# Turning half of a on VectorE in 32x32 blocks instead of on TensorE, in a fused matmul-GELU-matmul

## The chip, the core and the metric

The kernel runs on one core of a Trainium2 chip. The metric is the device time of one execution in microseconds; below, "us" is always that. The core has a matrix engine (TensorE, PE in the profile, with its weight loads listed apart as PEld), a vector engine (VectorE, DVE), an activation engine (ScalarE, ACT), GpSimd (POOL) and SyncE (SP). Loads are issued by SyncE, which moves bytes as they are, or by GpSimd, which here also casts float32 to bfloat16 on the way. Each engine runs its own instructions in the order in which the program gives them.

## The reference

```python
def setup_inputs():
    m, k, n, p = 1024, 1024, 2048, 1024   # a: m x k, b: k x n, c: n x p, float32

def reference(a, b, c):
    h = np.matmul(a, b)
    h = 0.5 * h * (1 + np.tanh(np.sqrt(2 / np.pi) * (h + 0.044715 * h ** 3)))
    return np.matmul(h, c).astype(np.float32)
```

## The kernel before

The first product is computed transposed: h^T, 2048 rows in 16 tiles of 128, by 1024 columns in two halves of 512 (`h` = 0 and 1, rows 0 to 511 and 512 to 1023 of a). A product on TensorE takes a 128x128 block of b as weights (contraction row tile `k`, column tile `t`) and streams 512 columns of a transposed (`aT[:, h, k]`). Its partitions are the contraction, so a has to be turned: its contraction index must lie on the partitions.

Before the change, all of a is turned on TensorE. Four transposes of 128x128 make one 128x512 piece in PSUM, and VectorE copies it to `aT` (`turn`, L138 to L147). a comes in eight quarters (`h`, `q`): 512 rows by 256 columns, 512 KB of float32. Three of them, (0,0), (1,0) and (0,1), come as float32 on SyncE's queue and are cast by VectorE and ScalarE (`cast_a`); the other five come already cast on GpSimd's queue (`abq`, L86). b's first three row tiles come in the same way on SyncE's queue (`stb`, `cast_b`), the rest of b and all of c as bfloat16 on GpSimd's (L89 to L104). GpSimd's queue starts after a small gate instruction (L81) that waits for the first quarter of a.

The work falls into stages, written out by hand in one order for every engine (`manual_schedule`; nothing reorders it):

- The first stage (L229 to L287) computes h^T's column tiles 0 to 3, both halves, directly: `block(h, tiles, ks)` runs `mm1` (L112) over row tiles `ks`. The products of a row tile stand between the transposes of the next. Eight PSUM banks hold `ps[0, t]`, `ps[1, t]` and the transposes (`bank(7)`). When a half is summed, `gelu` on ScalarE writes it to `hT`.
- Then three rounds of one level of Strassen-Winograd's scheme (seven products for eight, class `Seven`, function `seven`, products on L212): `zero` (column tiles 4 to 7), `one` (8 to 15) and `two` (the second matmul with c). Their operands are sums and differences formed on VectorE (`t1` to `t4`, `s1` to `s4`, L170) in float32r. `zero.t1` needs row tiles 0 to 3 of `aT`, `zero.t2` and `zero.t3` row tiles 4 to 7; `zero.s1` needs columns 768 to 1023 of b, `b1[:, :, 768:]`, all eight row tiles.
- `zero`'s first products take `b1[:, 0:4]`, columns from 512 on, its second products `b1[:, 4:8]`; those columns are loaded by L98.

Slots are shared: `x1`, `x2`, `x3` hold staging tiles first and Strassen operands later.

Of the kernel before, what the change touches and what calls it, by code (L numbers as in the profile page):

```python
# [9 lines left out]
F32 = mybir.dt.float32  # L10
F32R = mybir.dt.float32r
BF16 = mybir.dt.bfloat16
AF = mybir.ActivationFunctionType
# [6 lines left out]
def kernel(ctx, tc, a, b, c, out):  # L20
    nc = tc.nc
# [3 lines left out]
    H = 512  # L25
    KT = K // 128
    NT = N // 128

    av = a.rearrange("(mt p) k -> p mt k", p=128)
    bv = b.rearrange("(kt p) n -> p kt n", p=128)  # L30
    cv = c.rearrange("(nt p) q -> p nt q", p=128)

    ctx.enter_context(tc.manual_schedule())
# [6 lines left out]
    def slot(tag, shape, dt, name):  # L40
        return big.tile(shape, dt, name=name, tag=tag)

    def bank(i, shape=(128, H), dt=F32, name="ps"):
        return pp.tile(list(shape), dt, name=name, tag=f"bank{i}", padded_shape=None)

    def pieces(tag, bufs, shape, dt, name):
        return small.tile(shape, dt, name=name, tag=tag, bufs=bufs)
# [4 lines left out]
    gate = consts.tile([128, 1], F32, name="gate")  # L52
    g = consts.tile([128, 1], F32, name="g")
# [5 lines left out]
    aT = slot("a", [128, 2, KT, H], BF16, "aT")  # L59
    b1 = slot("b1", [128, KT, 1024], BF16, "b1")  # L60
    b2 = slot("b2", [128, KT, 1024], BF16, "b2")
# [2 lines left out]
    KH = KT // 2  # L64
    stb = slot("x0", [128, KT, H], F32, "stb")
    sta = slot("x1", [128, 2, 2, 4, 256], F32, "sta")
    abq = slot("x3", [128, 4, 2, 4, 256], BF16, "abq")

    def a_part(h, q):
        return av[:, 4 * h:4 * h + 4, ds(q * 256, 256)]  # L70

    def b_part(q):
        return bv[:, 2 * q:2 * q + 2, 0:H]

    nc.sync.dma_start(out=sta[:, 0, 0], in_=a_part(0, 0))  # L75
    nc.sync.dma_start(out=stb[:, 0:2], in_=b_part(0))  # L76
    nc.sync.dma_start(out=sta[:, 1, 0], in_=a_part(1, 0))
    nc.sync.dma_start(out=sta[:, 0, 1], in_=a_part(0, 1))
    nc.sync.dma_start(out=stb[:, 2], in_=bv[:, 2, 0:H])

    nc.gpsimd.tensor_copy(gate, sta[:, 0, 0, 3, 0:1])  # L81
    nc.scalar.activation(g, warm[:, 0:1], AF.Gelu_apprx_tanh)


    def cast_load_a(h, q):
        nc.gpsimd.dma_start(out=abq[:, q, h], in_=a_part(h, q))  # L86

    def cast_load_b(q):
        nc.gpsimd.dma_start(out=b1[:, 2 * q:2 * q + 2, 0:H], in_=b_part(q))  # L89

    cast_load_a(1, 1)
    nc.gpsimd.dma_start(out=b1[:, 3, 0:H], in_=bv[:, 3, 0:H])
    for q in range(2, 4):
        cast_load_a(0, q)
        cast_load_b(q)
        cast_load_a(1, q)
    for k in range(0, KT, 4):
        nc.gpsimd.dma_start(out=b1[:, k:k + 4, H:], in_=bv[:, k:k + 4, ds(H, H)])  # L98
    for n in range(2):
        for k in range(0, KT, 4):  # L100
            nc.gpsimd.dma_start(out=b2[:, k:k + 4, ts(n, H)],
                                in_=bv[:, k:k + 4, ds(1024 + n * H, H)])
    for t in range(0, NT, 2):
        nc.gpsimd.dma_start(out=c_sb[:, t:t + 2], in_=cv[:, t:t + 2])  # L104

    def copy(eng, dst, src):
        if eng is nc.scalar:
            nc.scalar.activation(dst, src, AF.Copy)
        else:
            nc.vector.tensor_copy(dst, src)  # L110

    def mm1(p, t, h, ks):  # L112
        for k in ks:
            nc.tensor.matmul(p, b1[:, k, ts(t, 128)], aT[:, h, k],  # L114
                             start=(k == 0), stop=(k == KT - 1))

    def gelu(t, h, p):
        nc.scalar.activation(hT[h][:, t], p, AF.Gelu_apprx_tanh)  # L118

    ps = {(0, t): bank(t) for t in range(4)}  # L120
# [7 lines left out]
    def cast_a(h, q, *engs):  # L128

        ab = pieces("ab", 2, [128, 4, 256], BF16, "ab")  # L130
        for i, eng in enumerate(engs):
            w = 256 // len(engs)
            for j, e in enumerate(eng if isinstance(eng, tuple) else (eng,)):
                m = slice(2 * j, 2 * j + 2) if isinstance(eng, tuple) else slice(0, 4)
                copy(e, ab[:, m, ts(i, w)], sta[:, h, q][:, m, ts(i, w)])
        return ab

    def turn(h, q, i, ab):  # L138

        banks = i if isinstance(i, tuple) else (i,)  # L140
        pts = [bank(x, (128, 2, H), BF16, "pt") for x in banks]
        for n in range(2):
            pt = pts[n % len(pts)]
            for m in range(4):
                nc.tensor.transpose(pt[:, n, ts(m, 128)], ab[:, m, ts(n, 128)], ident)  # L145
            nc.vector.tensor_copy(aT[:, h, 2 * q + n], pt[:, n])  # L146
            yield  # L147

    def cast_b(k, *engs):
        c0 = 0  # L150
        for i, eng in enumerate(engs):
            w = (H - c0) if i == len(engs) - 1 else H // len(engs) // 128 * 128
            copy(eng, b1[:, k, ds(c0, w)], stb[:, k, ds(c0, w)])
            c0 += w

    def block(h, tiles, ks):
        for k in ks:
            for t in tiles:
                mm1(ps[h, t], t, h, (k,))
# [56 lines left out]
    def pair(i):  # L216
        x = slot(f"x{i}", [128, 2, 4, H], F32R, "x1")
        return x[:, 0], x[:, 1]
# [3 lines left out]
    def quarters(b, c0, w):  # L222
        return [[b[:, 0:4, ds(c0, w)], b[:, 4:8, ds(c0, w)]],
                [b[:, 0:4, ds(c0 + w, w)], b[:, 4:8, ds(c0 + w, w)]]]

    zero = Seven(4, quarters(b1, H, 256), BB, [None] * 4, [None] * 4, 2)
    one = Seven(4, quarters(b2, 0, H), BB, [None] * 4, zero.t)

    stir(256, 256, 256, 256, 256)  # L229
    tn = turn(0, 0, 4, cast_a(0, 0, nc.vector))  # L230
    next(tn)
    stir(128)
# [4 lines left out]
    ab = cast_a(1, 0, nc.vector, nc.scalar)  # L237
    block(0, range(4), (0,))
    block(0, range(2), (1,))
    for _ in turn(1, 0, (7, 6), ab):  # L240
        pass
    block(0, range(2, 4), (1,))
    ab = cast_a(0, 1, (nc.scalar, nc.vector), nc.vector)
# [3 lines left out]
    zero.t[0], zero.t[1] = pair(2)  # L247
    block(1, range(3), (0,))
    tn = turn(0, 1, 7, ab)
    next(tn)  # L250
    block(1, range(3), (1,))
    next(tn)
    zero.t1(4, 0)
    for q in range(1, 3):
        k = 2 * q
        block(0, range(4), (k,))
        tn = turn(1, q, 7, abq[:, q, 1])
        next(tn)
        block(0, range(4), (k + 1,))
        next(tn)  # L260
        zero.t1(4, q)
        block(1, range(3), (k,))
        tn = turn(0, q + 1, 7, abq[:, q + 1, 0])
        next(tn)
        block(1, range(3), (k + 1,))
        next(tn)
    zero.t1(4, 3)
    block(0, range(4), (6, 7))
    zero.t2(2, 0)
    for t in range(4):  # L270
        gelu(t, 0, ps[0, t])
    ps[1, 3] = bank(7)
    mm1(ps[1, 3], 3, 1, range(2))
    tn = turn(1, 3, 0, abq[:, 3, 1])
    next(tn)
    mm1(ps[1, 3], 3, 1, range(2, 5))
    next(tn)
    mm1(ps[1, 3], 3, 1, (5,))
    zero.t[2], x11 = pair(1)
    zero.t[3], x31 = pair(3)  # L280
    zero.plain_t(2, 0)
    zero.t3(2, 0)
    zero.t2(2, 1)
    block(1, range(3), (6, 7))
    mm1(ps[1, 3], 3, 1, range(6, 8))
    for t in range(4):
        gelu(t, 1, ps[1, t])  # L287

# [199 lines left out]
```

## Time and profile before

| | |
|---|---|
| median of 3 runs | 117.67 us (117.56 to 117.71) |
| span of the profiled execution, first to last instruction | 115.7 us |
| what lies around the span, if the profiled execution took the median | 2.0 us |
| TensorE busy | 111.1 us (96%), 542 matmuls and transposes |
| VectorE busy | 90.0 us (78%) |
| ScalarE busy | 51.4 us (44%) |
| granted TensorE clock | 1.00 |
| loads by GpSimd (q0) | 9.31 MB as bfloat16, 8672 packets |
| loads by SyncE and all stores (q1) | 6.56 MB, 4736 packets |

How to read it: the span runs from the first to the last instruction. "Busy" of TensorE counts pipelined matmuls, so 96% isn't 96% of peak. A line such as `L146 DVE COPY aT<-pt 128x512 bf16<-128x512 bf16 x16 | 6.7, 423` names the line of the program, the engine, the operation, the tile written and the tile read with their shapes, how many there are, their busy time in us and the mean of one in ns. The chain of waits follows the work that ended last back from the end, at each step to what released it; in order of time each of its lines is a start in us, a length in us and what it was. In the timeline each line is a start, a length, an instruction (or several alike), and in brackets how long the engine had been idle and what ended that. An answer for one source line gives durations in ns (smallest, median, largest), the first and last start in us, and for a load the time from issue to landing.

### The profile page before, as it was taken

The page shows a single profiled execution, that of the slowest core. Times are in us where ns is not written, and L with a number is a line of the kernel's source. Part 1 is how long each engine was busy: PE and PEld are TensorE (multiplying, and loading weights), DVE is VectorE, ACT ScalarE, POOL GpSimd, SP SyncE. Part 2 cuts the span into 40 slices and gives each one's busy share as a digit, 9 for nine tenths or more (in the row PEclk, how much of TensorE's full clock was granted, in tenths as well). Part 3 has the DMA queues.
Part 4 walks back from the last instruction along what each step waited for, and adds up shares of the span by engine and source line. Part 5 has one row for each costly group of instructions (what it writes and reads, how often), then busy time and mean ns, then how long its engine had stood idle before and what let it go on. Part 6 is the DMA issues. An engine that isn't in the chain of part 4 may idle for free.

```text
span 115.7 us, 1461 instructions
## 1 busy us (share of the span) xinstructions
PE 111.1 (96%) x542; PEld 77.1 (67%) x542; DVE 90.0 (78%) x107; ACT 51.4 (44%) x86; POOL 17.2 (15%) x29
## 2 busy tenths in 40 slices
PE   7989999999999999999999999999999999999980
PEld 6645555546776447888885444688888888888860
DVE  0347748789999998935699999999999986954770
ACT  5053000999259997166698429500124982000000
POOL 2497755223322000000000000000000000000000
PEclk9999999999999999999999999999999999999999
DMA  2999999999999999998000000060000002014993
GB/s 69 295 381 229 200 199 205 204 208 205 206 211 209 212 213 209 212 210 168 8 0 0 6 0 0 38 235 0 0 0 0 0 4 91 1 73 176 370 363 106
DMA packets 13414, 15.94 MB, mean 138 GB/s; under 512 B 736, under 2 KB 9312, under 8 KB 13408
## 3 DMA queue, kind: packets, MB, share of 16 engines
q0 software_dynamic: 8672, 9.31, 47.6%
q1 hardware_dynamic: 4736, 6.56, 15.8%
q8 instruction: 4, 0.07, 0.3%
q14 instruction: 2, 0.02, 0.0%
HBM read 20.97 MB, written 4.19 MB: 218 GB/s over the span
## 4 chain that ended last, share of the span: by engine, by line
PE 90%; DMA 5%; SPq 1%; DVE 1%; issue 0%
PE ps L212 76%; PE ps L114 11%; DMA sta<-in_a_dram 5%; PE pt L145 3%; SPq L76 0%; DVE ab L110 0%; SPq L75 0%; DVE ot L375 0%
## 5 line engine op out<-in xcount | busy, mean ns | idle before, releaser
L212 PE MATMUL ps<-x,s 128*128 128x512 f32 x128 | 29.6, 391 | 0.0
L212 PEld LDWEIGHTS ps<-x,s 128*128 128x128 f32 x128 | 24.0, 188 | 5.1
L212 PE MATMUL ps<-x,x 128*128 128x512 f32 x96 | 22.9, 394 | 0.0
L212 PEld LDWEIGHTS ps<-x,x 128*128 128x128 f32 x96 | 18.0, 188 | 3.9
L114 PE MATMUL ps<-aT,b 128*128 128x512 bf16 x64 | 16.1, 379 | 0.2 <-DVE b L110 0.2
L298 ACT ACTIVATE v<-ps 128x512 f32<-128x512 f32 x10 | 6.0, 599 | 19.1 <-PE ps L212 19.1
L212 PE MATMUL ps<-c_sb,hT 128*128 128x512 bf16 (+1 forms) x72 | 14.2, 356 | 0.0
L212 PE MATMUL ps<-x 128*128 128x512 f32 x56 | 13.2, 392 | 0.0
L212 PEld LDWEIGHTS ps<-x 128*128 128x128 f32 x56 | 10.2, 188 | 2.6 <-ACT u L298 0.4
L118 ACT ACTIVATE hT<-ps 128x512 bf16<-128x512 f32 x14 | 7.3, 595 | 9.7 <-PE ps L114 9.7
L212 PEld LDWEIGHTS <-hT 128*128 128x128 bf16 x72 | 6.9, 98 | 7.0 <-issue 0.5
L118 ACT ACTIVATE hT<-ot 128x512 bf16<-128x512 f32 x18 | 10.4, 624 | 2.0 <-DVE ot L303 2.0
L212 PE MATMUL ps<-aT,b 128*128 128x512 bf16 x48 | 10.7, 379 | 0.0
L146 DVE COPY aT<-pt 128x512 bf16<-128x512 bf16 x16 | 6.7, 423 | 5.1 <-PE pt L145 5.1
L303 DVE TENSOR_TENSOR ot<-ps,u 128x512 f32<-128x512 f32 x10 | 6.7, 690 | 5.1 <-ACT u L298 5.1
L303 DVE TENSOR_TENSOR ot<-ps,v 128x512 f32<-128x512 f32 x10 | 6.7, 688 | 4.8 <-DMA out_dram<-ot 3.8
L170 DVE TENSOR_TENSOR x<-c_sb 128x1024 fp32r<-128x1024 bf16 x8 | 9.3, 1226 | 0.0
L114 PEld LDWEIGHTS <-b 128*128 128x128 bf16 x64 | 5.7, 98 | 4.5 <-DVE b L110 0.3
L212 PEld LDWEIGHTS <-b 128*128 128x128 bf16 x48 | 4.6, 98 | 5.7 <-issue 0.3
L104 POOL DMA_DIRECT2D c_sb<-in_c_dram x8 | 5.6, 702 | 13.1 <-DMA b<-in_b_dram 12.4
L170 DVE TENSOR_TENSOR x<-b 128x1024 fp32r<-128x1024 bf16 (+1 forms) x4 | 7.0, 1752 | 0.6 <-issue 0.6
L298 ACT ACTIVATE u<-ps 128x512 f32<-128x512 f32 x10 | 5.9, 598 | 3.4 <-PE ps L212 3.2
(44 smaller groups left out, 111.3 us busy)
## 6 DMA issues: line engine op xcount, KB each, us to landing
c_sb<-in_c_dram POOLq DMA_DIRECT2D x8, 512.0 KB, 20.0
out_dram<-ot SPq DMA_DIRECT2D x13, 256.0 KB, 2.1
b<-in_b_dram POOLq DMA_DIRECT2D x6, 512.0 KB, 15.3
sta<-in_a_dram SPq DMA_DIRECT2D x3, 512.0 KB, 6.1
abq<-in_a_dram POOLq DMA_DIRECT2D x5, 256.0 KB, 7.9
out_dram<-ot SPq DMA_DIRECT2D x6, 128.0 KB, 2.0
stb<-in_b_dram SPq DMA_DIRECT2D x1, 512.0 KB, 5.3
b<-in_b_dram POOLq DMA_DIRECT2D x2, 256.0 KB, 8.2
```

The lines of the kernel that those rows point to most:

```text
L104: nc.gpsimd.dma_start(out=c_sb[:, t:t + 2], in_=cv[:, t:t + 2])
L114: nc.tensor.matmul(p, b1[:, k, ts(t, 128)], aT[:, h, k], start=(k == 0), stop=(k == KT - 1))
L118: nc.scalar.activation(hT[h][:, t], p, AF.Gelu_apprx_tanh)
L145: nc.tensor.transpose(pt[:, n, ts(m, 128)], ab[:, m, ts(n, 128)], ident)
L146: nc.vector.tensor_copy(aT[:, h, 2 * q + n], pt[:, n])
L170: nc.vector.tensor_tensor(out=dst[:, r], in0=x[:, r], in1=y[:, r], op=op)
L212: nc.tensor.matmul(p[:, ds(c0, w)], l[:, k, ts(j, 128)], r[:, k, ds(c0, w)], start=(start and k == 0), stop=(k == self.kt - 1), skip_group ...
L298: nc.scalar.activation(st, p, AF.Copy)
L303: nc.vector.tensor_tensor(out=ot, in0=p, in1=st, op=ADD)
```

## The change

The contraction's lower half (row tiles 0 to 3) is turned on TensorE as before. The upper half (columns 512 to 1023 of a) is turned by VectorE, which transposes 32x32 blocks inside groups of 32 partitions. A's columns 512 + 128 d to 512 + 128 d + 127 are loaded into partitions 32 d to 32 d + 31, one DMA for each `d`, with the row within a block of 32 on the partition. VectorE then transposes every fourth column (`every4`), which puts column 512 + 4 p + s of a on partition p. Row tile 4 + s of b is loaded to match: partition p gets row 512 + 4 p + s (`bw`).

Half 0 of these columns comes as float32 on SyncE's queue (`wide`, four DMAs of 32 partitions, 16 runs of 512 bytes each); VectorE transposes it in float32 and ScalarE casts it (`square_wide`). Half 1 comes cast on GpSimd's queue (`low`, eight DMAs of 32 partitions), and VectorE transposes it in bfloat16 straight to `aT` (`square`). Quarter (1,1) of a and b's row tile 3 move from GpSimd's queue to SyncE's. The gate of GpSimd's queue now waits for b's row tile 2. Half 1's upper products are made in two column halves of 256.

```diff
+    bw = b.rearrange("(g p s) n -> p g s n", g=2, s=4)
+    aw = a.rearrange("(h t p) k -> p h t k", h=2, p=32)
...
-    abq = slot("x3", [128, 4, 2, 4, 256], BF16, "abq")
+    wide = slot("x3", [128, 32, 128], F32, "wide")
+    low = wide[:, 16:24].rearrange("p t k -> p (t k)").bitcast(BF16).rearrange("p (t k) -> p t k", k=128)
...
+    def b_rows(k, n, c0):
+        rows = bv[:, k:k + n] if k < 4 else bw[:, 1, k - 4:k - 4 + n]
+        return rows[:, :, ds(c0, H)]
...
+    nc.sync.dma_start(out=sta[:, 1, 1], in_=a_part(1, 1))
+    nc.sync.dma_start(out=stb[:, 3], in_=bv[:, 3, 0:H])
+    for d in range(4):
+        nc.sync.dma_start(out=wide[ts(d, 32), 0:16], in_=aw[:, 0, :, ds(512 + 128 * d, 128)])
-    nc.gpsimd.tensor_copy(gate, sta[:, 0, 0, 3, 0:1])
+    nc.gpsimd.tensor_copy(gate, stb[:, 2, 0:1])
...
+    def cast_load_a(t0, n):
+        for g in range(4):
+            nc.gpsimd.dma_start(out=low[ts(g, 32), ds(t0, n)],
+                                in_=aw[:, 1, ds(t0, n), ds(512 + 128 * g, 128)])
+    cast_load_b(b1, 4, 2, 0)
+    cast_load_b(b1, 6, 2, 0)
+    cast_load_a(0, 8)
+    cast_load_a(8, 8)
+    for k in range(0, KT, 2):
+        cast_load_b(b1, k, 2, H)
...
+    def every4(x, k):
+        return x.rearrange("p t (k s) -> p t k s", s=4)[:, :, :, k]
+    def square_wide():
+        for k in range(4):
+            f = pieces("ab", 2, [128, 16, 32], F32, "f")
+            nc.vector.transpose(f, every4(wide[:, 0:16], k))
+            nc.scalar.activation(aT[:, 0, 4 + k].rearrange("p (t m) -> p t m", m=32), f, AF.Copy)
+    def square(t0, n):
+        for k in range(4):
+            nc.vector.transpose(aT[:, 1, 4 + k, ds(32 * t0, 32 * n)].rearrange("p (t m) -> p t m", m=32),
+                                every4(low[:, ds(t0, n)], k))
...
-    for q in range(1, 3):
-        k = 2 * q
-        block(0, range(4), (k,))
-        tn = turn(1, q, 7, abq[:, q, 1])
-        next(tn)
-        block(0, range(4), (k + 1,))
-        next(tn)
-        zero.t1(4, q)
-        block(1, range(3), (k,))
-        tn = turn(0, q + 1, 7, abq[:, q + 1, 0])
-        next(tn)
-        block(1, range(3), (k + 1,))
-        next(tn)
-    zero.t1(4, 3)
-    block(0, range(4), (6, 7))
-    zero.t2(2, 0)
+    ab = cast_a(1, 1, (nc.scalar, nc.vector), nc.vector)
+    cast_b(3, nc.scalar, nc.scalar)
+    block(0, range(4), (2,))
+    tn = turn(1, 1, 7, ab)
+    next(tn)
+    block(0, range(4), (3,))
+    next(tn)
+    for i in range(1, 4):
+        zero.t1(4, i)
+    block(1, range(3), (2, 3))
+    square_wide()
+    ps[1, 3] = bank(7)
+    mm1(ps[1, 3], 3, 1, range(4))
+    block(0, range(4), range(4, KT))
+    square(0, 8)
     for t in range(4):
         gelu(t, 0, ps[0, t])
-    ps[1, 3] = bank(7)
-    mm1(ps[1, 3], 3, 1, range(2))
-    tn = turn(1, 3, 0, abq[:, 3, 1])
-    next(tn)
-    mm1(ps[1, 3], 3, 1, range(2, 5))
-    next(tn)
-    mm1(ps[1, 3], 3, 1, (5,))
+    square(8, 8)
     zero.t[2], x11 = pair(1)
     zero.t[3], x31 = pair(3)
+    zero.t2(2)
     zero.plain_t(2, 0)
     zero.t3(2, 0)
-    zero.t2(2, 1)
-    block(1, range(3), (6, 7))
-    mm1(ps[1, 3], 3, 1, range(6, 8))
+    for r in range(2):
+        for k in range(4, KT):
+            for t in range(4):
+                mm1(ps[1, t], t, 1, (k,), slice(256 * r, 256 * r + 256))
```

More of the change, by code (lines that the diff above doesn't have):

```diff
@@ L66 @@
     sta = slot("x1", [128, 2, 2, 4, 256], F32, "sta")
-    abq = slot("x3", [128, 4, 2, 4, 256], BF16, "abq")
+    wide = slot("x3", [128, 32, 128], F32, "wide")
+    low = wide[:, 16:24].rearrange("p t k -> p (t k)").bitcast(BF16).rearrange("p (t k) -> p t k", k=128)
     def a_part(h, q):
         return av[:, 4 * h:4 * h + 4, ds(q * 256, 256)]
-    def b_part(q):
-        return bv[:, 2 * q:2 * q + 2, 0:H]
+    def b_rows(k, n, c0):
+        rows = bv[:, k:k + n] if k < 4 else bw[:, 1, k - 4:k - 4 + n]
+        return rows[:, :, ds(c0, H)]
     nc.sync.dma_start(out=sta[:, 0, 0], in_=a_part(0, 0))
-    nc.sync.dma_start(out=stb[:, 0:2], in_=b_part(0))
+    nc.sync.dma_start(out=stb[:, 0:2], in_=b_rows(0, 2, 0))
     nc.sync.dma_start(out=sta[:, 1, 0], in_=a_part(1, 0))
@@ L79, with cast_load_b @@
     nc.sync.dma_start(out=stb[:, 2], in_=bv[:, 2, 0:H])
-    nc.gpsimd.tensor_copy(gate, sta[:, 0, 0, 3, 0:1])
-    nc.scalar.activation(g, warm[:, 0:1], AF.Gelu_apprx_tanh)
[L85 to L98, printed above, removed]
+    nc.sync.dma_start(out=sta[:, 1, 1], in_=a_part(1, 1))
[3 more added lines that the diff above has]
+    nc.gpsimd.tensor_copy(gate, stb[:, 2, 0:1])
+    nc.scalar.activation(g, warm[:, 0:1], AF.Gelu_apprx_tanh)
+    def cast_load_a(t0, n):
+        for g in range(4):
+            nc.gpsimd.dma_start(out=low[ts(g, 32), ds(t0, n)],
+                                in_=aw[:, 1, ds(t0, n), ds(512 + 128 * g, 128)])
+    def cast_load_b(tile_, k, n, c0):
+        nc.gpsimd.dma_start(out=tile_[:, k:k + n, ds(c0 % 1024, H)], in_=b_rows(k, n, c0))
+    cast_load_b(b1, 4, 2, 0)
[4 more added lines that the diff above has]
+        cast_load_b(b1, k, 2, H)
     for n in range(2):
         for k in range(0, KT, 4):
-            nc.gpsimd.dma_start(out=b2[:, k:k + 4, ts(n, H)],
-                                in_=bv[:, k:k + 4, ds(1024 + n * H, H)])
+            cast_load_b(b2, k, 4, 1024 + n * H)
     for t in range(0, NT, 2):
@@ L110, in copy, with mm1 @@
             nc.vector.tensor_copy(dst, src)
-    def mm1(p, t, h, ks):
+    def mm1(p, t, h, ks, r=slice(0, H)):
         for k in ks:
-            nc.tensor.matmul(p, b1[:, k, ts(t, 128)], aT[:, h, k],
-                             start=(k == 0), stop=(k == KT - 1))
+            nc.tensor.matmul(p[:, r], b1[:, k, ts(t, 128)], aT[:, h, k, r],
+                             start=(k == 0), stop=(k == KT - 1 and r.stop == H))
     def gelu(t, h, p):
```

## The prediction

> **What bounds the kernel now.** I read the chain of waits first, as shares and then in order of time, to see which stage the change can move.
>
> ```profile
> PE 90%; DMA 5%; SPq 1%; DVE 1%; issue 0%
> ...
> 11.22 0.86 PE ps L114 x4
> 12.09 0.22 PE pt L145 x4
> 12.31 0.86 PE ps L114 x4
> ...
> 22.26 0.25 PE pt L145 x4
> 22.51 1.94 PE ps L114 x9
> 24.46 87.96 PE ps L212 x400
> ```
>
> From 8.4 us on, TensorE alone carries the chain. Until 24.3 us it mixes products of a and b (L114, 0.86 us for four, 0.216 each) with transposes of a (L145, 0.22 to 0.25 us for four). From there the Strassen products (L212) run back to back. So the change is worth what it does to the time at which L212 starts, plus any new wait soon after. The second view is the timeline of VectorE, which shows its order around the first stage.
>
> ```profile
> 11.26 0.42 DVE L146 COPY aT<-pt 128x512 bf16<-128x512 bf16 x1 [0.47 <-PE pt L145]
> 11.60 0.68 DVE L170 TENSOR_TENSOR x<-aT 128x512 fp32r<-128x512 bf16 x1
> ...
> 13.44 0.42 DVE L146 COPY aT<-pt 128x512 bf16<-128x512 bf16 x1 [0.66 <-PE pt L145]
> ...
> 19.61 0.68 DVE L170 TENSOR_TENSOR x<-aT 128x512 fp32r<-128x512 bf16 x1
> 20.21 1.22 DVE L170 TENSOR_TENSOR x<-aT,x 128x1024 fp32r<-128x1024 bf16 x1
> ...
> 25.80 1.23 DVE L170 TENSOR_TENSOR x<-b 128x1024 fp32r<-128x1024 bf16 x1 [0.56 <-issue]
> ```
>
> A 128x512 difference holds VectorE 0.60 us (19.61 to 20.21), though it is written as 0.68. The first four `t1` parts stand spread over idle time here. Third, the landings of SyncE's loads, line by line, and of GpSimd's first:
>
> ```profile
> L77 SPq DMA_DIRECT2D sta<-in_a_dram x1: 462/462/462, 1.8 to 1.8; - x1
> DMA to landing us min/median/max: 6.1/6.1/6.1
> L78 SPq DMA_DIRECT2D sta<-in_a_dram x1: 507/507/507, 2.3 to 2.3; - x1
> DMA to landing us min/median/max: 7.0/7.0/7.0
> L79 SPq DMA_DIRECT2D stb<-in_b_dram x1: 551/551/551, 2.8 to 2.8; - x1
> DMA to landing us min/median/max: 7.1/7.1/7.1
> L92 POOL DMA_DIRECT2D b<-in_b_dram x1: 548/548/548, 5.9 to 5.9; - x1
> DMA to landing us min/median/max: 5.9/5.9/5.9
> ```
>
> By issue plus landing, L77 is in at 7.9 us, L78 at 9.3, L79 at 9.9: 512 KB in 1 KB runs costs 1.4 us, 256 KB in 2 KB runs 0.6. GpSimd's loads, issued from 5.1 us on, land only after SyncE's last one (L92 at 11.85), and then the queue moves some 200 GB/s of bfloat16 without a gap: 512 KB of it per 2.6 us. I read that as GpSimd's queue standing behind SyncE's.
>
> **What it removes.** Eight sets of four transposes on TensorE: 8 x 0.235 = 1.9 us of the chain. Their eight copies out of PSUM leave VectorE. The 32 half-wide products that replace 16 full ones cost nothing: the 128x256 bf16 matmuls at the kernel's end run 16 in 1.92 us, the last one's 0.27 us included, so 0.11 us each, half of 0.216. The relabelled contraction (row 512 + 4p + s of b against every fourth column of a) costs no instruction, and the b loads keep their 2 KB runs.
>
> **What it adds before a's upper half is needed.** By its timeline TensorE comes to the transposes of a's quarter (1,1) at 11.93 us. That quarter now comes as float32 on SyncE's queue behind L79: 9.9 + 1.4 = 11.3 us. Its casts on VectorE stand behind `t1` (11.60 to 12.2) and the first takes 0.28 us: 12.5. So TensorE waits **0.6 us** here, for an order on VectorE that the program fixes. b's row tile 3 lands at 11.3 + 0.6 = 11.9, and ScalarE's two casts of 0.41 (L108 row) come in time.
>
> The second copy out of PSUM then ends at 14.4. Behind it VectorE has three `t1` parts, 3 x 0.60, until 16.2; only then the first transpose of `wide` can start. TensorE has work without it until 16.1: 18 products from 11.06 (3.9 us), two sets of transposes (0.5), and the 0.6. **So even with all data there it waits for one transpose and one ScalarE cast.** No row has a transpose. [...] ScalarE's cast of 128x512 is 0.63. 16.2 + 1.3 = 17.5: a wait of 1.4 to 1.5 us.
>
> [...]
>
> **When `wide` lands.** It starts at 11.9 behind the rest of SyncE's queue; the six further issues (0.5 us each, done by 6.7 us) are hidden by that queue. 1 MB in 512 B runs: by bytes 2 x 1.4 = 2.8 us (14.7), by runs 2048 against L77's 512, 4 x 1.4 = 5.6 us (17.5). Rows speak for bytes as far as the length of the run goes (2 KB to 1 KB cost only 15%). But each of the four fills only 32 partitions, and every load in this trace fills 128; no row shows that, and it can only hurt. I take three quarters of the way, 4.9 us: **16.8 us**, 0.6 to 0.7 later than VectorE is free.
>
> [...]
>
> **The sum at the end of the stage.** First product of the upper half at 16.85 + 0.69 + 0.63 = 18.2, a wait of 2.1 us; b's tiles 4 and 5, first on GpSimd's queue after SyncE's, land at 16.85 + 1.3 = 18.15, just in time. -1.9 + 0.6 + 2.1 = **+0.8 to 0.9 us**: L212 starts at about 25.2. Moving GpSimd's gate to a later load (first issue about 10.7 instead of 5.1) is hidden while its queue stands behind SyncE's; were the two served side by side instead, b's two loads ahead of it would push `wide` back by up to 2.6 us, and the wait with it. The granted clock is 1.00 in every slice; what a gap of 2 us does to it no row shows, and I take nothing for it.
>
> **What comes after.** GpSimd's queue goes on: tiles 6 and 7 at 19.5, `low` (1 MB of float32, 0.5 MB of bf16, by the 200 GB/s) at 20.8 and 22.2. VectorE's eight transposes of 128x256 hold it 0.34 each (the 128x256 difference's 0.42, less the 0.08 by which the next starts early): until 22.2 and 23.5. The two column halves end at 23.4 and 25.2, so these hide. b's next columns, 1 MB of bf16, then land at 24.8 and 27.4; before, by L98's issues and landings, at 23.1 and 25.8. TensorE wants the second half of them at 25.2 + 1.7 = 26.9: **another 0.5 us**. The 25.80 row (`s1`) needs them too: 27.4, ends 28.6, before the products that read it at 29.1. Four more GpSimd issues (26 for 22) of 0.7 us lie beside transfers; it waits with eight loads under way, so the last two pieces of `low` and b's columns may each slip by a few tenths: 0 to 0.8 us, in the range only. Loads of c keep 3 us to spare (VectorE reads c from 59.7 us, the last load lands at about 56, and both move). ScalarE's four casts lie in its 9.7 us of idle time before the first gelu.
>
> Total +1.4 us. The sum stands against the profiled execution: span 115.7 us, with 2.0 us around it if it took the median of 117.67: 117.1 + 2.0 = **119.1 us**.
>
> **The rivals.**
> - *`wide` lands by bytes, 14.7 us.* Then VectorE's `t1` queue decides alone: -1.9 + 0.6 + 1.5 = +0.2, and b's columns come at 25.3, no further wait: 117.9. For it: run length hardly mattered so far. Against: 32 partitions. Chance 0.22, around the border of no change.
> - *The strided transposes are slow.* At 1.22 and 0.69, VectorE needs 4 x 1.14 + 8 x 0.60 = 9.4 us from 16.85, until 26.2; then `t2` (2.3), `t3` (1.1) and `s1` (1.2) end at 30.8 where TensorE would need it at 29.1: +1.7 more, 120.8. For it: a step of 16 bytes that no row shows. Chance 0.18. [...]
> - *Faster.* It is decided at one place, the first product of the upper half: it has to start before 17.1 us. [...] Against it: the 0.6 and the `t1` queue are in the program's order. Chance 0.14.
> - *It doesn't do what it says* (TensorE still turning the upper half): excluded, the diff takes those calls out.
>
> **How the numbers follow.** Forecast 0.46. Range: from the faster rival's 117.4 to the slow transposes' 120.8, with a little for GpSimd's slips, 120.9; left out are a stronger gain and both mishaps together, under 2 in 10. What a measurement can tell from no change is about 0.2% (0.24 us). Of the bytes case I count half as slower: slower 0.46 + 0.18 + 0.11 = 0.75, within 0.2% 0.11, faster 0.14.
>
> **What would show it.** The changed profile should have 32 transposes on TensorE instead of 64; a wait of TensorE of about 0.6 us near 12 us and one of about 2 us before its first upper product (18.2); `wide`'s last landing near 16.8; transposes of about 0.69 and 0.42; L212 from about 25.2. A start of L212 before 24 us, or `wide` landing past 18, would break the forecast.

## The result, and the profile after

The changed kernel takes 122.27 us (median of four), the kernel before in the same comparison 117.62: a ratio of 1.039, 95% interval 1.037 to 1.041. The forecast was 119.1 us, with 117.4 to 120.9 as its range: the direction was right, the size was not. (Here and in some of the runs below one or two executions lie well above the rest; the ratios leave those out.)

The chain of waits, as shares and then in order of time:

```profile
PE 72%; DMA 20%; POOL 3%; SPq 2%; issue 1%; DVE 0%
...
10.31 0.76 POOL b L102
11.07 8.32 DMA b<-in_b_dram
19.39 0.28 issue
19.68 0.58 POOL wide L98
20.25 2.12 POOL b L102 x3
22.37 8.50 DMA b<-in_b_dram
30.87 0.05 issue
30.92 86.29 PE ps L238 x390
```

Before, TensorE carried it from 8.4 us on. Now GpSimd's queue does, until 30.9 us: a load of b (L102), a wait for its landing, an issue of a piece of `low` (L98, written to the tile `wide`), then the load of b's columns for the second products. L238 is L212 of before. TensorE's timeline shows when each step came:

```profile
12.70 0.29 PE L155 MATMUL pt<-ident,ab 128*128 128x128 bf16 x2 [0.35 <-DVE ab L120]
14.23 2.35 PE L124 MATMUL ps<-aT,b 128*128 128x512 bf16 x10
19.32 8.79 PE L124 MATMUL ps<-aT,b 128*128 128x512 bf16 x48 [2.75 <-ACT aT L167]
27.95 2.32 PE L238 MATMUL ps<-aT,b 128*128 128x512 bf16 x10
30.92 1.47 PE L238 MATMUL ps<-aT,b 128*128 128x512 bf16 x6 [0.64 <-DMA b<-in_b_dram]
```

First upper product at 19.3 (forecast 18.2), L238 from 27.95 (25.2), the last six of the second products held until 30.9 (27.4). The lines of VectorE and GpSimd say why it is late in each place:

```profile
14.77 1.88 DVE L196 TENSOR_TENSOR x<-aT 128x512 fp32r<-128x512 bf16 x3
17.53 4.02 DVE L166 STREAM_TRANSPOSE f<-wide 128x512 f32<-128x512 f32 x4 [0.88 <-DMA wide<-in_a_dram]
21.48 2.68 DVE L172 STREAM_TRANSPOSE aT<-wide 128x256 bf16<-128x256 bf16 x8
```

```profile
11.79 3.60 POOL L98 DMA_DIRECT2D wide<-in_a_dram  x6
18.41 0.58 POOL L98 DMA_DIRECT2D wide<-in_a_dram  x1 [3.02 <-DMA b<-in_b_dram]
19.68 0.58 POOL L98 DMA_DIRECT2D wide<-in_a_dram  x1 [0.69 <-DMA b<-in_b_dram]
20.24 5.81 POOL L102 DMA_DIRECT2D b<-in_b_dram  x8
```

GpSimd issues eight loads, then waits 3.0 us for the first to land and 0.69 us for the second, and issues b's columns only after that. In the table of stages (busy time of each engine, then granted clock, share of the DMA engines, GB/s) the queue then runs thin, and the clock has gone down:

```profile
18.00:19.00 1.00, 0.00 (x0) 0.10 (x1) 1.00 (x2) 0.36 (x1) 0.58 (x1) 1.00 1.60 182
21.00:22.00 1.00, 1.00 (x4) 0.41 (x3) 1.00 (x3) 0.65 (x2) 1.00 (x2) 0.50 1.09 98
22.00:23.00 1.00, 1.00 (x4) 0.30 (x2) 1.00 (x4) 0.21 (x1) 1.00 (x2) 0.50 1.02 108
23.00:24.00 1.00, 1.00 (x5) 0.45 (x4) 1.00 (x4) 0.00 (x0) 1.00 (x3) 0.88 1.04 133
```

98 to 133 GB/s from 21 to 24 us, and TensorE at half clock after idling 2.75 us. The kernel before moved 205 to 208 in the same stretch:

```profile
21.00:23.00 2.00, 2.00 (x17) 1.13 (x15) 1.30 (x4) 1.87 (x4) 0.00 (x0) 1.00 1.24 205
23.00:25.00 2.00, 2.00 (x11) 0.94 (x10) 2.00 (x2) 1.98 (x4) 0.70 (x1) 1.00 1.25 208
```

Which of these sets the time, the experiments had to say.

### The profile page after: what moved, and what is told of

Read it like the earlier page. It is cut to its first block, busy times and chain, and to the rows that moved or that the text cites. A ratio compares the mean times of both kernels' runs of the same rounds, so it can differ in the third digit from the quotient of the medians.

```text
span 120.7 us, 1465 instructions
## 1 busy us (share of the span) xinstructions
PE 112.3 (93%) x526; PEld 77.4 (64%) x526; DVE 93.6 (78%) x113; ACT 54.7 (45%) x93; POOL 18.6 (15%) x33
## 4 chain that ended last, share of the span: by engine, by line
PE 72%; DMA 20%; POOL 3%; SPq 2%; issue 1%; DVE 0%
PE ps L238 72%; DMA b<-in_b_dram 14%; DMA stb<-in_b_dram 6%; POOL b L102 2%; POOL wide L98 0%; SPq L83 0%; SPq L81 0%; SPq L82 0%; SPq L80 0%; DVE ot L396 0%; POOL gate L91 0%
## 5 line engine op out<-in xcount | busy, mean ns | idle before, releaser
L238 PE MATMUL ps<-x,s 128*128 128x512 f32 x128 | 29.6, 391 | 0.0
L238 PEld LDWEIGHTS ps<-x,s 128*128 128x128 f32 x128 | 24.0, 188 | 5.1
L238 PE MATMUL ps<-x,x 128*128 128x512 f32 x96 | 22.7, 392 | 0.0
L238 PEld LDWEIGHTS ps<-x,x 128*128 128x128 f32 x96 | 17.9, 188 | 4.2 <-issue 0.4
L124 PE MATMUL ps<-aT,b 128*128 128x512 bf16 (+1 forms) x80 | 16.7, 362 | 2.9 <-ACT aT L167 2.7
L238 PE MATMUL ps<-c_sb,hT 128*128 128x512 bf16 (+1 forms) x72 | 14.2, 356 | 0.0
L124 PEld LDWEIGHTS <-b 128*128 128x128 bf16 x80 | 8.0, 103 | 9.3 <-issue 3.0
L238 PE MATMUL ps<-x 128*128 128x512 f32 x56 | 13.3, 394 | 0.0
L238 PEld LDWEIGHTS ps<-x 128*128 128x128 f32 x56 | 10.1, 188 | 2.8 <-ACT u L319 0.4
L238 PE MATMUL ps<-aT,b 128*128 128x512 bf16 x48 | 10.9, 379 | 0.6 <-DMA b<-in_b_dram 0.6
L238 PEld LDWEIGHTS <-hT 128*128 128x128 bf16 x72 | 6.9, 98 | 7.0 <-issue 0.5
L238 PEld LDWEIGHTS <-b 128*128 128x128 bf16 x48 | 4.5, 97 | 6.4 <-DMA b<-in_b_dram 1.1
L102 POOL DMA_DIRECT2D b<-in_b_dram x10 | 7.4, 756 | 0.0
```

The lines of the kernel that those rows point to most:

```text
L102: nc.gpsimd.dma_start(out=tile_[:, k:k + n, ds(c0 % 1024, H)], in_=b_rows(k, n, c0))
L124: nc.tensor.matmul(p[:, r], b1[:, k, ts(t, 128)], aT[:, h, k, r], start=(k == 0), stop=(k == KT - 1 and r.stop == H))
L238: nc.tensor.matmul(p[:, ds(c0, w)], l[:, k, ts(j, 128)], r[:, k, ds(c0, w)], start=(start and k == 0), stop=(k == self.kt - 1), skip_group ...
```

## The experiments

Two theories stood first. The queue theory: GpSimd's queue, held back twice with eight loads under way, brings b's columns late, and everything else hides behind it. The clock theory: TensorE's late and slow products set the time. All edits are to the changed kernel unless said otherwise.

**1. The gate put back.**

```diff
-    nc.gpsimd.tensor_copy(gate, stb[:, 2, 0:1])
+    nc.gpsimd.tensor_copy(gate, sta[:, 0, 0, 3, 0:1])
```

> The changed kernel with GpSimd's gate put back on the first quarter of a, so that GpSimd issues its first loads from about 5 us instead of 10.3. If GpSimd's queue stands behind SyncE's anyway and its last two pieces of a wait for landings (queue theory), its first data still flow at about 15 us and the time stays at 122.3 (within 0.4). If the later gate itself is the cause of the late columns of b, they land several us earlier and the time falls to 119.5 or less.

Measured: 127.84 us, ratio 1.088 (1.083 to 1.094): neither. SyncE's loads behind b's row tile 2 now move beside GpSimd's (213 to 215 GB/s for both together from 16 to 22 us), and `wide` is not usable before 23 us. VectorE's timeline there:

```profile
22.99 4.02 DVE L166 STREAM_TRANSPOSE f<-wide 128x512 f32<-128x512 f32 x4 [2.60 <-DMA wide<-in_a_dram]
```

So my reading that GpSimd's queue stands behind SyncE's was wrong. In the trace before, its first load landed at 11.3 us, after SyncE's last (9.9); here its first has landed by 12.3 us (when GpSimd goes on issuing), with the last of SyncE's in at 22.8. The later gate is not a cost of the change but something it needs.

**2. Fewer loads on GpSimd's queue.**

```diff
-    cast_load_a(0, 8)
-    cast_load_a(8, 8)
-    for k in range(0, KT, 2):
-        cast_load_b(b1, k, 2, H)
+    cast_load_a(0, 16)
+    for k in range(0, KT, 4):
+        cast_load_b(b1, k, 4, H)
```

> The changed kernel with the casting loads of a in four DMAs instead of eight and b's next columns in two instead of four, so that the first eight loads of GpSimd's queue cover all that the first stage and the next products need. Queue theory (GpSimd held back twice with eight loads under way, so the queue ran dry near 21 us): b's second columns land at about 27.7 instead of 30.9, the second products no longer wait, the time falls by 1.2 us, to 121.0, and TensorE's late start (27.9) then bounds it. Clock theory (only TensorE's late and slow products count): no change, 122.3.

Measured: 120.59 us, ratio 1.024 (1.019 to 1.029). The queue theory had 121.0, and the time fell as it said; the size fits only loosely, since it rests on executions at 119.9, 120.1 and 121.1, the last at a clock of 0.98. The stages are read in run 4, which has the same edits and those of run 3.

**3. TensorE kept busy while it waits.** Six products of zeros, added to a sum that is under way:

```diff
     mm1(ps[1, 3], 3, 1, range(4))
+    for i in range(6):
+        nc.tensor.matmul(ps[1, 3][:, 0:256], warm[:, 0:128], warm,
+                         start=False, stop=False, skip_group_check=True)
```

> The changed kernel with six products of zeros (0.4 us each) into a bank under accumulation while TensorE waits for the upper half, so that it never idles there. They add nothing to the result. Queue theory: the clock is granted in full, L238's first products start about 1.5 us earlier, but they then wait for b's columns at 30.9 and the time stays at 122.3. Clock theory: the time falls by 1.5 to 2 us, to about 120.5.

Measured: 122.30 us, no change, at a clock of 1.00. Its TensorE:

```profile
26.78 0.59 PE L238 MATMUL ps<-aT,b 128*128 128x512 bf16 x2
28.24 1.90 PE L238 MATMUL ps<-aT,b 128*128 128x512 bf16 x8 [0.86 <-DMA b<-in_b_dram]
30.80 1.47 PE L238 MATMUL ps<-aT,b 128*128 128x512 bf16 x6 [0.67 <-DMA b<-in_b_dram]
```

The full clock brings L238 forward by 1.2 us (27.95 to 26.78), and b's columns take it all back: the last six of the second products start at 30.8, as in the changed kernel (30.9). In the changed kernel the queue decides, and the half clock is hidden.

**4. Both edits.**

> Both edits together: four and two DMAs on GpSimd's queue, and products of zeros while TensorE waits. Queue and clock theory together: 1.2 us from the queue and a further 1.5 from the clock, about 119.6; what then remains over before (2 us) is the late landing of the 32-partition loads and the float32 transposes. If the time stays above 120.8, a third cause is missing.

Measured: 120.56 us, ratio 1.026 (1.023 to 1.028), 1.0 above what was expected. Its stages from 22 us, and TensorE's timeline:

```profile
22.00:24.00 2.00, 1.64 (x10) 0.72 (x9) 0.84 (x3) 1.54 (x4) 2.00 (x4) 1.00 1.26 207
24.00:26.00 2.00, 2.00 (x21) 1.79 (x19) 2.00 (x7) 0.82 (x3) 0.79 (x2) 1.00 1.24 206
```

```profile
23.66 3.65 PE L123 MATMUL ps<-aT,b 128*128 128x256 bf16 x32 [0.36 <-DVE aT L171]
27.15 3.62 PE L237 MATMUL ps<-aT,b 128*128 128x512 bf16 x16
```

The queue keeps 206 to 207 GB/s, and the 16 products follow without a break: b's columns no longer hold them. Of the 1.0, the trace shows 0.36 as a wait for the cast load of a, which, now in one piece, is usable only at 23.2 and holds the column halves. A further 0.3 was expected too much of the clock (1.5, where run 3 showed 1.2); the rest was not taken apart.

**5. One edit of the queue at a time.** The cast loads of a in four DMAs (first), or b's columns in two (second):

```diff
-    cast_load_a(0, 8)
-    cast_load_a(8, 8)
+    cast_load_a(0, 16)
```

> The changed kernel with one edit: the cast loads of a in four DMAs of 16 blocks instead of eight of 8; b's next columns stay in four. If it is the eight small loads that use up the eight places under way, GpSimd's queue no longer runs dry before b's columns, they move at 200 GB/s from first to last, and the time is that of the two edits on the queue together, 120.6. If the four pieces of b's columns are what is slow, they stay at 100 to 170 GB/s and the time stays near 122.

```diff
-    for k in range(0, KT, 2):
-        cast_load_b(b1, k, 2, H)
+    for k in range(0, KT, 4):
+        cast_load_b(b1, k, 4, H)
```

> The changed kernel with the other edit alone: b's next columns in two DMAs of 512 KB instead of four of 256 KB, the cast loads of a in eight as they were. If running dry is what slows the queue down afterwards, the last two loads of a still wait for landings, the queue still runs dry near 21 us, b's columns come at 100 to 170 GB/s, and the time stays at 121.6 to 122.4. If the small pieces are slow, it falls to 120.6.

Measured: 121.39 us (1.0325, 1.031 to 1.034) and 121.60 us (1.034, 1.033 to 1.036). By time alone they can't be told apart; the traces can. First the one with four loads of a, then the one with b's columns in two, 22 to 24 us:

```profile
22.00:24.00 2.00, 2.00 (x14) 1.14 (x12) 1.48 (x5) 1.54 (x4) 1.57 (x4) 1.00 1.24 205
```

```profile
22.00:24.00 2.00, 2.00 (x10) 0.86 (x9) 2.00 (x8) 0.34 (x2) 2.00 (x4) 0.91 0.97 139
```

With four loads of a the queue keeps its rate; with eight it runs thin whatever the size of b's pieces. The eight small loads are the cause of that. The first of the two also prices the clock by itself, since it is no longer hidden: its one execution at a clock of 1.00 took 120.1 us, the other four, at 0.980 to 0.985, took 121.1 to 121.5. The trace of the one at 1.00 shows the wait before its upper products, 2.72 us:

```profile
19.41 7.53 PE L123 MATMUL ps<-aT,b 128*128 128x512 bf16 x48 [2.72 <-ACT aT L166]
```

The lower clock costs **1.0 to 1.4 us** where TensorE is the bound, and whether it comes differs from run to run. The other four have no trace; that they lost their time to the clock is read from their mean clocks. In the second kernel, where the queue still decides, the clock is worth nothing: 121.7 us at 1.00, 121.2 to 121.6 at 0.983 to 0.986.

**6. Where 32 partitions matter.** The same bytes in the same 512-byte runs, over 128 partitions:

```diff
-        nc.sync.dma_start(out=wide[ts(d, 32), 0:16], in_=aw[:, 0, :, ds(512 + 128 * d, 128)])
+        nc.sync.dma_start(out=wide[:, 4 * d:4 * d + 4], in_=av[:, 0:4, ds(512 + 128 * d, 128)])
```

> The changed kernel with the float32 load of a's upper columns over all 128 partitions: the same bytes, the same four DMAs and 512-byte runs, but other elements (the output is not the reference's). If the 32 partitions set its pace, it moves at 300 to 390 GB/s and its last landing comes at 15 us; if the length of the runs does, it stays at 210 to 230 GB/s and lands near 17.2 as in the changed kernel. The time itself should hardly move, since GpSimd's queue bounds it.

Measured: 120.88 us (one execution). The stage from 13 to 14 us, where hardly anything but `wide` moves (455 of 455 packets are of SyncE's queue in the changed kernel, 683 of 689 here), first in the changed kernel, then here:

```profile
13.00:14.00 1.00, 0.87 (x4) 0.41 (x5) 0.42 (x1) 0.38 (x2) 1.00 (x3) 1.00 1.24 227
```

```profile
13.00:14.00 1.00, 1.00 (x10) 0.54 (x8) 0.34 (x2) 0.00 (x0) 1.00 (x2) 1.00 1.17 345
```

227 against 345 GB/s: the 32 partitions set the pace. The short runs cost little: the kernel before moved 348 GB/s from 5 to 8 us, all of it on SyncE's queue, in runs of 1 and 2 KB. `wide` then no longer holds VectorE (its first transpose starts at 16.1, when the `t1` differences are done). The time fell by 1.4 us, which I had not expected: GpSimd's first load lands sooner (GpSimd stops waiting for it at 16.7 instead of 18.4), and b's columns come at 29.3.

**7. Where the step matters.** On top of both edits of run 4, the float32 transposes read adjacent columns:

```diff
-            nc.vector.transpose(f, every4(wide[:, 0:16], k))
+            nc.vector.transpose(f, wide[:, 4 * k:4 * k + 4].rearrange("p t (u m) -> p (t u) m", m=32))
```

> The kernel of the queue and clock edits together, with the float32 transposes reading 32 adjacent columns instead of every fourth (the output is not the reference's). If the step of 16 bytes makes them 1.06 us, they fall to about 0.65 to 0.69 each; if float32 itself does, they stay. The time stays at about 120.5, since that kernel waits for the cast load of a next.

Measured: 120.68 us (one execution), so the time stays, as expected. The answers for that line, in the changed kernel and here, in ns:

```profile
L166 DVE STREAM_TRANSPOSE f<-wide x4: 1045/1060/1081, 17.5 to 20.5; 128x512 f32<-128x512 f32 x4
```

```profile
L165 DVE STREAM_TRANSPOSE f<-wide x4: 669/690/712, 17.4 to 19.5; 128x512 f32<-128x512 f32 x4
```

0.69 us is what the forecast took; reading every fourth float32, 16 bytes apart, costs 0.37 more. In bfloat16, 8 bytes apart, no such price shows: 0.394 for 256 elements in the changed kernel and 0.669 for 512 in the next run, no more than adjacent float32. No run has adjacent bfloat16 to compare.

**8. The float32 half undone.** Both halves come cast on GpSimd's queue (`cast_load_a(h)` now loads half `h` in four DMAs):

```diff
-    for d in range(4):
-        nc.sync.dma_start(out=wide[ts(d, 32), 0:16], in_=aw[:, 0, :, ds(512 + 128 * d, 128)])
-    nc.gpsimd.tensor_copy(gate, stb[:, 2, 0:1])
+    nc.gpsimd.tensor_copy(gate, sta[:, 1, 0, 3, 0:1])
...
+    cast_load_a(0)
+    cast_load_b(b1, 4, 4, 0)
+    cast_load_a(1)
+    for k in range(0, KT, 4):
+        cast_load_b(b1, k, 4, H)
...
-            f = pieces("ab", 2, [128, 16, 32], F32, "f")
-            nc.vector.transpose(f, every4(wide[:, 0:16], k))
-            nc.scalar.activation(aT[:, 0, 4 + k].rearrange("p (t m) -> p t m", m=32), f, AF.Copy)
+            nc.vector.transpose(aT[:, 0, 4 + k].rearrange("p (t m) -> p t m", m=32), every4(low[:, 0:16], k))
```

> The changed kernel with the float32 half undone: both halves of a's upper columns come cast on GpSimd's queue (four DMAs each, b's tiles 4 to 7 in one and its next columns in two), VectorE transposes both in bfloat16 without a cast by ScalarE, and the gate is on a's quarter (1,0). No load of 32 partitions stands on SyncE's queue any more and the first transposes can start when VectorE is free, about 16.2 us. Expected: upper products from 17, L238's from about 25, b's second columns at 26.2, the time 118.4. If the half on SyncE's queue was not what costs, it stays above 120.

Measured: ratio 1.009 (1.007 to 1.012), resting on two of the four executions, 118.5 and 118.8 us. Of the 4.6 us all but about 1.1 is gone. The run also has larger cast loads and an earlier gate, so it does not price the float32 half by itself. Its TensorE:

```profile
17.87 7.31 PE L120 MATMUL ps<-aT,b 128*128 128x512 bf16 x48 [1.43 <-DMA b<-in_b_dram]
25.01 3.62 PE L232 MATMUL ps<-aT,b 128*128 128x512 bf16 x16
```

**9. What was on offer.** The kernel before, with its loads untouched, without the upper half's transposes and their copies; the lower half is read in their place:

```diff
-            nc.tensor.matmul(p, b1[:, k, ts(t, 128)], aT[:, h, k],
+            nc.tensor.matmul(p, b1[:, k, ts(t, 128)], aT[:, h, k % 4],
```

> The kernel before without the eight sets of transposes of the upper half and their copies: products and differences read the lower half of a in their place (the output is not the reference's), all loads stay as they were. It gives what the removal can bring when nothing is put in its place. If TensorE alone bounded the stage: 1.9 us less, 115.6. If the loads stand just behind TensorE (b's columns for the second products land at 25.8, wanted then at 24.1): the second products wait for them, and the time falls by 0.2 to 0.4 us only, to about 117.2.

Measured: 117.32 us, ratio 0.997 (0.995 to 0.999). Its TensorE:

```profile
18.66 4.92 PE L114 MATMUL ps<-aT,b 128*128 128x512 bf16 x22 [0.76 <-DMA b<-in_b_dram]
23.41 1.89 PE L212 MATMUL ps<-aT,b 128*128 128x512 bf16 x8
26.00 1.90 PE L212 MATMUL ps<-aT,b 128*128 128x512 bf16 x8 [0.70 <-DMA b<-in_b_dram]
```

1.9 us of TensorE's work taken away, with nothing in its place, is worth 0.3 us. The second products wait for b's columns until 26.0, which is when they started anyway.

**10. A version meant to win.** Run 8, with b's tiles 4 and 5 in a load of their own and the `t1` differences behind the first four transposes:

```diff
-    cast_load_b(b1, 4, 4, 0)
+    cast_load_b(b1, 4, 2, 0)
+    cast_load_b(b1, 6, 2, 0)
...
-    zero.t1(4, 0)
...
-    for i in range(1, 4):
-        zero.t1(4, i)
     block(1, range(3), (2, 3))
     square_wide()
+    for i in range(4):
+        zero.t1(4, i)
```

> A version meant to win: both halves cast on GpSimd's queue as in the run before, b's tiles 4 and 5 in a load of their own so that the upper products start at about 16.2 instead of 17.9, and VectorE's four t1 differences moved behind the first four transposes, which takes away the 0.6 us at 12 us and the wait for them. TensorE then waits about 1.3 us for half 1, L238's products start at about 24.4 and b's second columns land about 25.8: 117.5, no more than 0.2 from before, because the loads bound both. If TensorE's order alone counted, it would be 116.5.

Measured: ratio 1.009 (1.007 to 1.010), median 118.61 us: no better than run 8, 1.1 above what was expected. The profiled execution took 120.47 us, 1.9 above the median, so its stages don't stand for the others; why the reordering brought nothing stays open.

**11. All four costs taken out together**, runs 2, 3, 6 and 7 in one kernel:

> All four costs taken out of the changed kernel at once: the two edits on GpSimd's queue, the products of zeros, the float32 load over 128 partitions, and transposes of adjacent columns (the output is not the reference's; the work is the same in number and size). If these four are the whole account, the first upper product starts at about 17.5, L238's at about 24.4, b's second columns land about 25, and the time is 117.7, the kernel before's within 0.4, not 1.9 below it, because the loads bound the end of the stage. If it stays above 118.5, something else costs too.

Measured: 119.00 us, ratio 1.012 (1.009 to 1.014): 3.3 us less than the changed kernel, 1.3 more than expected. The six products of zeros, sized for a wait until 19.3, now outlast it and hold the first upper product back until 18.7, where 17.5 was expected; that is 1.2 of the 1.3:

```profile
16.12 2.77 PE L293 MATMUL ps<-const-float32-0.0 128*128 128x256 f32 x12
18.73 7.11 PE L123 MATMUL ps<-aT,b 128*128 128x512 bf16 x47
```

`low` stands close behind. It is usable at 21.4, which TensorE doesn't wait for here; without the zeros it would have wanted it at about 21 (17.5 and 16 products of 0.216, my estimate):

```profile
21.44 2.73 DVE L171 STREAM_TRANSPOSE aT<-wide 128x256 bf16<-128x256 bf16 x8 [2.45 <-DMA wide<-in_a_dram]
```

## Why the prediction was right or wrong

- *TensorE's wait at 12 us*, forecast 0.6: the products behind these transposes start at 13.13 where they would have started at about 12.3, so 0.8. Right in kind and nearly in size.
- *The `t1` differences in front of the transposes*: they end at 16.6 (forecast 16.2). Right, and with `wide` over 128 partitions they become what holds VectorE, as the first rival had it.
- *`wide` at 16.8*: VectorE got it at 17.5. The choice towards the slow end of the two bounds was right, and run 6 shows that its ground, the 32 partitions, was the right one. From 12 to 15 us, where SyncE's queue alone moves, this trace has 211 to 227 GB/s; over 128 partitions run 6 has 346 and 345 from 12 to 14.
- *Transposes at 0.69*: 1.06 in float32. No run shows 0.69 for a float32 transpose of every fourth column; run 7 has it for adjacent columns (0.690). I had made slow transposes a rival, at up to 1.22, with chance 0.18, and its second half, 0.69 for the bfloat16 transposes, did not come true (0.39). Of the 1.1 us by which the first upper product is later than forecast, 0.4 is this and 0.7 `wide`. The range's lower end, 117.4, needed the first upper product at 17.1 (16.2 + 0.28 + 0.63) and so a 128x512 transpose of 0.28, which no run shows; the fastest is 0.67 (runs 7 and 8).
- *The clock*: put at nothing, because no row showed a gap. It stood at 0.50 for about 3.4 us after a wait of 2.75 us. Shown in run 5 as 1.0 to 1.4 us where TensorE bounds; worth nothing in the changed kernel itself, by run 3.
- **The step that failed** is the slip of GpSimd's queue, put at "0 to 0.8 us, in the range only". The last two pieces of `low` were issued 3.0 us and 0.7 us late, b's columns only behind them at 20.2, and the queue moved no more than 98 to 184 GB/s from 20 to 27 us: the last of the second products could start at 30.9, where the forecast had b's columns in at 27.4. That is 3.5 us, and it covers the whole gap between the forecast +1.4 and the measured 4.65. It does not stand alone: L238's own start, 27.95 for 25.2, is close behind. So larger loads alone bring the time to 120.6 to 121.4 (runs 2 and 5), and only with `wide`, the transposes and the clock mended as well does it come to 119.0 (run 11). I had the limit of eight loads in view (in the trace before, too, GpSimd issues eight, from 5.1 us on, and then waits 0.61 us for the first to land) and counted the loads, but took each piece for a few tenths of transfer, and never set the time of issue against the time at which the queue would be empty. By my reckoning, which no run shows step by step, the pieces are so small (64 KB as bfloat16, 0.37 us each at the 177 GB/s of 18 to 20 us) that six of them cover 2.2 us; a load that waits for a landing, takes 0.58 to issue and lands 2.7 us after its issue, as the quickest of the eight did, comes too late for that.
- *GpSimd's queue behind SyncE's*: wrong as a rule (run 1). The moved gate keeps the two mostly apart, so b's tiles 4 and 5 were in by 18.2, as forecast (18.15), but not for the reason given. Nor was it free: from 15.25 to 16.5 us both queues move, and SyncE's gets 220 packets through, which took it 0.5 us alone (1324 packets from 12 to 15). By my estimate `wide` is some 0.7 us later for it, the whole of its lateness.
- *What the removal is worth*: the sum credited 1.9 us. By run 9 it is worth 0.3 by itself, since b's columns come just when the second products start. The sum's end did not rest on the credit: it was set by b's columns, at 27.4.

What stays open is how the small loads slow the queue, and why it stays slow until 27 us although GpSimd issues one load after another from 20.2 on. From 22 to 24 us it does so in traces with eight small loads that were held back (121 GB/s in the changed kernel, 78 in run 3, 139 in run 5's second kernel), and not in those with four, on the changed kernel's order (204 to 207 in runs 2, 4 and 5's first); nor does it in run 1 (205), where eight were held back while SyncE's transfers went on. That the queue simply ran empty does not fit the table: from 21 to 24 us the DMA engines' share stays at 1.02 to 1.09 (1.24 before), while the rate halves. Nor is VectorE, busy without a gap there, the cause by itself: in run 5's first kernel it has no gap from 22.5 us on, at 205 to 206 GB/s from 22 to 26. Run 10's profiled execution, with a's cast loads in four DMAs a half, has a thin stretch too (130 GB/s from 17 to 19 us). No run took that apart.

## What to carry to other kernels

Before crediting the work that a change takes off the busiest engine, look for what lands just behind it: here the loads stood 0.3 us behind TensorE, and 1.9 us of its work was worth no more. When a change cuts a transfer into more and smaller loads, lay out each issue against the landing it has to wait for; here the loads late in the queue paid, not the ones that were cut (b's columns, issued from 20.2 us on, held the second products until 30.9). And the layout that suited VectorE's transpose had two prices of its own, to be read first: how many partitions each load fills (227 GB/s over 32, 345 over 128), and how far apart the transposed elements lie (1.06 us for 512 float32 elements 16 bytes apart, 0.69 for adjacent ones).

## What the runs showed of the hardware that I had not expected

- The 32x32 transposes on VectorE take about the same time in bfloat16 with a step of 8 bytes (0.394 us for 256 elements, 0.669 for 512) and in float32 with adjacent elements (0.690 for 512), but 1.06 us for 512 float32 elements 16 bytes apart.
- GpSimd's first load landed 6.2 us after its issue in the kernel before and 7.0 in run 1, where more of SyncE's loads follow; there it moves beside them, the last of them in at 22.8 us, and issuing it 5 us earlier than in the changed kernel cost 5.6 us in the end.
- After a wait of 2.75 us TensorE's granted clock stood at 0.50 for about 3.4 us; after one of 1.79 us in run 6 it stayed at 1.00. With nearly the same wait the two kernels of run 5 differ: 2.72 us left the clock at 1.00, 2.74 us halved it.
